# A masked softmax on one core: the first tile stored as three pieces (4, 4 and 8 rows per partition) instead of four (2, 2, 4 and 8)

## The chip, the core and the metric

The kernel runs on one core of a Trainium2 chip. The metric is the device time of one execution in microseconds: the median of several executions. A profiled execution gives a trace beside its time.

## The reference

The input `x` is 16 batches x 8 heads x 256 x 256 in float32; every batch has a length between 128 and 255. Each row is a softmax over its first `length` columns, and zero behind them.

```python
for b in range(batch):
    length = lengths[b]
    masked = x[b, :, :, :length].copy()
    masked = masked - np.max(masked, axis=-1, keepdims=True)
    exp_masked = np.exp(masked)
    result[b, :, :, :length] = exp_masked / np.sum(exp_masked, axis=-1, keepdims=True)
```

## The kernel before

A tile is one batch: 2048 rows of 256 floats, 16 rows in each of 128 partitions (`nt` = 16, `half` = 8, `quarter` = 4), 2 MB in all. A partition's 16 rows lie one behind the other in memory, in the input and in the output. Eight slots in SBUF (`xt`) hold tiles; position `b` in the order of work uses slot `b % 8`. There are 16 positions, 0 to 15. In this text a tile is named by its position (`batch_of`, L50, gives the batch).

Each tile goes through a load, a mask, an exponential with row sums, a division, and a store, in place:

- Loads. SP issues the load of tile 0 (L143). POOL issues those of tiles 1 to 3 as whole tiles (L194), and those of tiles 4 to 15 in a loop (L203, issue at L166), cut to a width that covers the batch's length, since the rest of the slot has been zeroed (L189). Before a load of the loop, POOL waits until the stores of the tile that had the slot are done (`s_st`, L207), and until the load two positions earlier has landed (`s_sw`, L165). So at most two of these loads are under way.
- Mask. VectorE takes the minimum of the data with a ramp that is far below zero behind the length (`clip`, L246). Tile 0 is masked in two halves, the others whole, so the third mask overall (`s_min` = 3) is that of tile 1.
- Exponential. ScalarE, one instruction for the first four rows (L372; VectorE sums these, L267), and one for each of the other twelve, which sums the row itself (L375).
- Division. VectorE takes reciprocals (L277) and multiplies, half a tile at a time (L280); each half raises `s_out` by 1.
- Store. SP, L144 to L154. `parts` (L59) cuts a tile into pieces, given in rows per partition. Every piece is one DMA of 128 partitions.

The order on VectorE is written out by hand (L287 to L300): both masks of tile 0, then for each tile the division of its first half, the mask of the next tile, the division of its second half, and the row sums of the next tile's first four rows. (For tile 1 the next mask comes first.) So the second half of tile `b` is divided after tile `b+1` has been masked, which needs the load of tile `b+1`.

SP runs through the stores in order. Before a piece it waits for the division of the half that holds the piece's last row (L147). Before the second piece of tile 0 it also waits for the third mask (L148, L149), and before the first piece of tiles 2 to 12 for the stores of the tile two positions earlier (L151). Behind the stores it waits for all of them (L155 to L157 and the end of the kernel). A store adds 16 for each piece of tile 0, and 16 for every four rows per partition of other tiles, so that each whole tile adds 64 (L154).

The last tiles: 13 and 14 are stored whole, 15 in two halves. Behind the last division VectorE checks that no sum was out of bounds (L315 to L326); a second pass that would repeat everything with the row maxima subtracted is not taken with these inputs.

Of the kernel before, what the change touches and what calls it, by code (L numbers as in the profile page):

```python
# [21 lines left out]
def kernel(  # L22
# [12 lines left out]
    nt = rows // P  # L35
    half = nt // 2
    quarter = nt // 4
# [12 lines left out]
    def batch_of(pos):  # L50
        return pos + 1 if pos < ahead - 1 else {ahead - 1: 15, 15: 0}.get(pos, pos)
# [7 lines left out]
    def parts(b):  # L59


        if b == 0:
            cuts = [0, 2, quarter, half, nt]
        elif b < 5:
            cuts = [0, half, half + quarter, nt]
        elif b < 13 or b == batch - 1:
            cuts = [0, half, nt]
        else:
            cuts = [0, nt]
        return [slice(i, j) for i, j in zip(cuts, cuts[1:])]  # L70
# [35 lines left out]
    with tc.tile_critical(sync_engine=POOL, no_gpsimd_drain=True):  # L106
# [37 lines left out]
        for b in range(batch):  # L144
            s_b = s_st[b % 2] if b < late else s_late if b < batch - 1 else s_last
            for s in parts(b):
                nc.sync.wait_ge(s_out, 2 * b + (s.stop - 1) // half + 1)  # L147
                if b == 0 and s.start == 2:  # L148
                    nc.sync.wait_ge(s_min, 3)  # L149
                if 2 <= b < late and s.start == 0:  # L150
                    nc.sync.wait_ge(s_b, 64 * (b // 2 + 2))  # L151
                nc.sync.dma_start(
                    out=out_f[batch_of(b), :, s, :], in_=xt[:, b % slots, s, :]
                ).then_inc(s_b, 16 * (1 if b == 0 else (s.stop - s.start) // quarter))  # L154
        for par in range(2):  # L155
            nc.sync.wait_ge(s_st[par], n_st[par])
        nc.sync.wait_ge(s_late, 64 * (batch - 1 - late))  # L157
# [45 lines left out]
        with nc.Fori(16, 16 * (batch // 2 - 1), 16, engines=[POOL]) as landed:  # L203
            for par in range(2):
                n = landed // 8 + (ahead - 2 + par)
                b = n % 15 if par == 1 else n
# [230 lines left out]
```

## Time and profile before

| what | value |
|---|---|
| median of 3 runs | 154.32 us (154.25 to 154.43) |
| the profiled execution | 154.43 us |
| its span in the trace | 152.8 us |
| VectorE busy | 134.7 us (88%) |
| ScalarE busy | 95.0 us (62%) |
| GpSimd (POOL) busy | 21.3 us (14%) |
| read from HBM, written to HBM | 27.98 MB, 33.55 MB |

The page has the busy time of each engine; a strip of 40 equal slices of the span, in which a digit is the busy share in tenths; the DMA queues (q1 is that of SP's transfers, q0 that of POOL's) with their packets, megabytes and the time of their packets as a share of 16 engines' time; and the transfers by size, with their count and, for loads, the median time from issue to landing. The rows of a queue can also be had for a stretch of the span alone; their share is then of 16 engines' time in that stretch. A timeline row has start, duration, engine, line, operation, and in brackets the idle time of the engine before it with what ended it. A row of a stretch (`a:b`) has its length, then for PE, weight loads, VectorE, ScalarE and POOL the busy time and the count of instructions, then the clock, the DMA share and GB/s. Times in the trace count from the start of the span.

### The profile page before, as it was taken

Reading aid. Unit: us, or ns where it says so; the run is one execution under the profiler, and the core shown is the slowest. Engines: PE = TensorE matmul, PEld = TensorE weight load, DVE = VectorE, ACT = ScalarE, POOL = GpSimd, SP = SyncE. Lnnn points to the kernel's source line nnn. Section 1 sums busy time; section 2 is a strip of 40 time slices with the busy share of each in tenths; the row PEclk is TensorE's granted clock in tenths of the full one; section 3 lists DMA queues with packets and bytes.
Section 4 is the critical chain, followed back from the end, with each engine's and each line's share of the span. In section 5 each row is a group of like instructions: output and inputs, shape, how many; then the busy total and the mean of one; then the engine's idle time right before and its main releaser. Section 6 shows DMA issues by size and latency. Waiting matters only on the chain.

```text
span 152.8 us, 817 instructions
## 1 busy us (share of the span) xinstructions
PE 0.3 (0%) x2; PEld 0.2 (0%) x2; DVE 134.7 (88%) x107; ACT 95.0 (62%) x402; POOL 21.3 (14%) x29
## 2 busy tenths in 40 slices
PE   0000000000000000000000000000000000000000
PEld 0000000000000000000000000000000000000000
DVE  1058999999999999999999999999999999889920
ACT  3019599808668493939486684939394866829200
POOL 4961110030303020030300303011030000000000
DMA  4999999999999999999999999999999999999993
GB/s 107 425 425 433 422 413 389 444 412 408 406 396 421 402 421 414 415 408 402 428 411 420 415 414 413 418 414 414 419 419 420 416 419 417 425 442 429 431 418 154
DMA packets 10070, 61.57 MB, mean 403 GB/s; under 512 B 834, under 2 KB 946, under 8 KB 6226
## 3 DMA queue, kind: packets, MB, share of 16 engines
q1 hardware_dynamic: 5328, 35.65, 56.7%
q0 software_dynamic: 4736, 25.89, 41.7%
q14 instruction: 4, 0.03, 0.1%
q10 hardware_dynamic: 2, 0.00, 0.0%
HBM read 27.98 MB, written 33.55 MB: 403 GB/s over the span
## 4 chain that ended last, share of the span: by engine, by line
DMA 82%; DVE 8%; issue 3%; POOL 1%; POOLq 1%; PE 0%; ACTq 0%
DMA xt<-in_x_dram 82%; DVE xt L280 5%; DVE xt L246 2%; POOL xt L189 1%; DMA word<-in_lengths_dram 1%; DVE row_sum L267 1%; POOLq L166 1%; DVE ends L315 0%; POOL xt L194 0%; DVE inv_sum L277 0%; DVE bad L318 0%; DVE len_s L237 0%; PE len_f L214 0%; PE count L216 0%; DVE len_b L234 0%
## 5 line engine op out<-in xcount | busy, mean ns | idle before, releaser
L375 ACT ACTIVATE xt<-xt 128x256 f32<-128x256 f32 x192 | 76.6, 400 | 0.0
L280 DVE TENSOR_TENSOR xt<-xt,inv_sum 128x2048 f32<-128x2048 f32 x32 | 73.4, 2292 | 1.1
L372 ACT ACTIVATE xt<-xt 128x1024 f32<-128x1024 f32 x16 | 16.9, 1057 | 45.7 <-DVE xt L246 45.7
L246 DVE SCALAR_TENSOR_TENSOR xt<-down,len_s,xt 128x2048 f32<-128x2048 f32 (+1 forms) x17 | 37.7, 2220 | 7.2 <-DMA xt<-in_x_dram 7.2
L375 ACT ACTIVATION_READ_ACCUMULATOR xt<-xt 128x1 f32 x192 | 35.9, 187 | 0.0
L166 POOL DMA_DIRECT2D xt<-in_x_dram x12 | 13.3, 1106 | 90.5 <-DMA xt<-in_x_dram 72.8
L267 DVE TENSOR_REDUCE row_sum<-xt 128x4 f32<-128x1024 f32 x16 | 19.4, 1212 | 0.0
L277 DVE RECIPROCAL inv_sum<-row_sum 128x8 f32<-128x8 f32 x32 | 6.4, 199 | 0.9 <-ACT xt L375 0.4
L189 POOL MEMSET xt<- 128x1536 f32 x4 | 5.4, 1398 | 1.1 <-DVE len_s L237 1.1
L359 ACT ACT_TABLE_LOAD x1 | 1.3, 1283 | 1.6 <-PEq L421 1.6
L194 POOL DMA_DIRECT2D xt<-in_x_dram x3 | 1.8, 591 | 0.0
L229 DVE TENSOR_SCALAR down<-iota_i 128x256 f32<-128x256 int32 x1 | 0.3, 301 | 1.6 <-POOL iota_i L179 1.6
L315 DVE TENSOR_REDUCE ends<-inv_sum 128x1 f32<-128x256 f32 x2 | 0.7, 408 | 0.0
L237 DVE TENSOR_SCALAR len_s<-len_f 128x16 f32<-128x16 f32 x1 | 0.2, 174 | 0.4 <-PE len_f L214 0.4
L216 PE MATMUL count<-bad,ones_c 128*1 128x3 bf16 x1 | 0.2, 165 | 143.4 <-DVE bad L318 143.4
L234 DVE CAST len_b<-word 1x16 bf16<-1x16 int32 x1 | 0.2, 163 | 0.4 <-DMA word<-in_lengths_dram 0.4
L179 POOL IOTA iota_i<- 128x256 int32 x1 | 0.3, 333 | 0.6 <-POOLq L106 0.6
L326 DVE TENSOR_REDUCE redo<-count 1x1 f32<-1x3 f32 x1 | 0.1, 150 | 0.3 <-PE count L216 0.3
L318 DVE TENSOR_SCALAR bad<-ends 128x1 bf16<-128x1 f32 x3 | 0.3, 150 | 0.0
L185 POOL MEMSET seed<- 1x1 f32 x2 | 0.2, 226 | 0.0
L216 PEld LDWEIGHTS count<-bad,ones_c 128*1 128x1 bf16 x1 | 0.1, 79 | 143.5 <-DVE bad L318 143.5
L359 ACT ACTIVATE warm<-const-float32-0.0 128x1 f32<-128x1 f32 x1 | 0.2, 203 | 0.0
(10 smaller groups left out, 1.1 us busy)
## 6 DMA issues: line engine op xcount, KB each, us to landing
out_dram<-xt SPq DMA_DIRECT2D x23, 1024.0 KB
xt<-in_x_dram POOLq DMA_DIRECT2D x4, 2048.0 KB, 16.5
xt<-in_x_dram POOLq DMA_DIRECT2D x3, 1728.0 KB, 18.2
out_dram<-xt SPq DMA_DIRECT2D x9, 512.0 KB
out_dram<-xt SPq DMA_DIRECT2D x2, 2048.0 KB
xt<-in_x_dram POOLq DMA_DIRECT2D x2, 1600.0 KB, 17.7
xt<-in_x_dram POOLq DMA_DIRECT2D x2, 1280.0 KB, 17.7
xt<-in_x_dram SPq DMA_DIRECT2D x1, 2048.0 KB, 8.2
```

What stands on the lines that cost most here:

```text
L166: nc.gpsimd.dma_start(out=xt[:, slot, :, :w], in_=x_n[:, b, :, :w]).then_inc(s_sw[par], 16)
L189: nc.gpsimd.memset(xt[:, b, :, low:], 0.0).then_inc(s_fill, 1)
L194: nc.gpsimd.dma_start(out=xt[:, b], in_=x_f[batch_of(b)]).then_inc(s_sw[b - 1] if b < 3 else s_ld[1], 16)
L216: nc.tensor.matmul(count, lhsT=ones_c, rhs=bad, start=True, stop=True).then_inc(s_count, 1)
L246: return nc.vector.scalar_tensor_tensor(out=t, in0=down[:, None, lo:hi].to_broadcast([P, s.stop - s.start, hi - lo]), scalar=len_s[:, batc ...
L267: nc.vector.tensor_reduce(out=row_sum[:, b % slots, :lump], in_=xt[:, b % slots, :lump, :], op=ALU.add, axis=AX,).then_inc(s_exp[0], 1)
L277: step(nc.vector.reciprocal(out=inv_sum[:, b, s], in_=row_sum[:, b % slots, s]))
L280: nc.vector.tensor_tensor(out=t, in0=t, in1=inv_sum[:, b, s, None].to_broadcast([P, half, seq_k]), op=ALU.mult,).then_inc(s_out, 1)
L315: step(nc.vector.tensor_reduce(out=ends[:, k : k + 1], in_=values, op=op, axis=AX))
L359: nc.scalar.activation(out=warm, in_=nc.const_aps.tensor(0.0, (P, 1), F32), func=EXP)
L372: nc.scalar.activation(out=e, in_=e, func=EXP).then_inc(s_lump, 1)
L375: ins = nc.scalar.activation(out=e, in_=e, func=EXP, accum_out=row_sum[:, slot, j : j + 1])
```

## The change

Tile 0 is cut at rows 4 and 8 instead of 2, 4 and 8: its first two pieces of 2 rows per partition (2 KB in each partition, 256 KB in all) become one piece of 4 rows (512 KB). The second piece, now rows 4 to 7, has the wait for the third mask that the piece from row 2 had. The semaphore's increments follow the general rule, so that tile 0 still adds 64. The instructions of the other engines are the same.

```diff
         if b == 0:
-            cuts = [0, 2, quarter, half, nt]
+            cuts = [0, quarter, half, nt]
...
-                if b == 0 and s.start == 2:
+                if b == 0 and s.start == quarter:
                     nc.sync.wait_ge(s_min, 3)
...
-                ).then_inc(s_b, 16 * (1 if b == 0 else (s.stop - s.start) // quarter))
+                ).then_inc(s_b, 16 * ((s.stop - s.start) // quarter))
```

## The prediction

> **What bounds the kernel now.** I read the page's DMA strip, queues and transfers first, then the DMA queues in chosen stretches, then the timeline of the last 20 us.
>
> ```profile
> span 152.8 us, 817 instructions
> DMA  4999999999999999999999999999999999999993
> DMA packets 10070, 61.57 MB, mean 403 GB/s; under 512 B 834, under 2 KB 946, under 8 KB 6226
> q1 hardware_dynamic: 5328, 35.65, 56.7%
> q0 software_dynamic: 4736, 25.89, 41.7%
> xt<-in_x_dram POOLq DMA_DIRECT2D x3, 1728.0 KB, 18.2
> xt<-in_x_dram SPq DMA_DIRECT2D x1, 2048.0 KB, 8.2
> out_dram<-xt SPq DMA_DIRECT2D x23, 1024.0 KB
> out_dram<-xt SPq DMA_DIRECT2D x9, 512.0 KB
> out_dram<-xt SPq DMA_DIRECT2D x2, 2048.0 KB
> out_dram<-xt SPq DMA_DIRECT2D x2, 256.0 KB
> ```
>
> The 16 DMA engines are full from the first slice to the last. q1 carries what SP issues: the first load and 36 stores, 37 transfers. 5328 / 37 = 144 packets each, for pieces of 256 KB and of 2048 KB alike: one per partition (128) and 16 small ones, one per DMA engine. So an engine's share of any SP transfer is 8 data packets and 1 small one, nine in all, whatever its size; a 2-row piece has packets of 2 KB, a 16-row piece of 16 KB. How do the queues share an engine? From 20 to 132 us, when both have work:
>
> ```profile
> q1 hardware_dynamic: 4373, 25.68, 55.7%
> q0 software_dynamic: 4350, 20.65, 45.8%
> ```
>
> 4373 packets against 4350, though the bytes differ by a quarter. It holds where the store packets are small (24 to 26 us, first pair below) and where they are large (124 to 129 us, second pair):
>
> ```profile
> q0 software_dynamic: 120, 0.57, 72.9%
> q1 hardware_dynamic: 121, 0.24, 30.5%
> ...
> q1 hardware_dynamic: 174, 1.29, 62.5%
> q0 software_dynamic: 172, 0.79, 39.8%
> ```
>
> The queues take turns packet by packet, and neither runs dry. So when the loads end depends on how many load packets there are, and on how large the store packets are that get the turns in between. The end of the loads matters here:
>
> ```profile
> DVE xt L246 <- DMA xt<-in_x_dram: 7.2, 2, 6.4
> 131.02 2.29 DVE L280 TENSOR_TENSOR xt<-xt,inv_sum 128x2048 f32<-128x2048 f32 x1
> 134.12 2.35 DVE L246 SCALAR_TENSOR_TENSOR xt<-down,len_s,xt 128x2048 f32<-128x2048 f32 x1 [0.81 <-DMA xt<-in_x_dram]
> 136.62 2.29 DVE L280 TENSOR_TENSOR xt<-xt,inv_sum 128x2048 f32<-128x2048 f32 x1
> 138.94 0.36 SPq L152 DMA_DIRECT2D out_dram<-xt  x1
> 142.63 0.36 SPq L152 DMA_DIRECT2D out_dram<-xt  x1
> 145.07 0.36 SPq L152 DMA_DIRECT2D out_dram<-xt  x1
> ```
>
> VectorE waits for loads twice, 6.4 us for the first tile and 0.81 us for the last one. The mask of tile 15 starts as its load lands, at 134.12. In VectorE's order it stands ahead of the second half of tile 14's division (136.62 to 138.91), and tile 14 is stored in one piece, issued at 138.94. So 134.12 + 4.82 = 138.94 is a chain without slack: last load, mask, division, store of tile 14. Is the store queue still supplied then?
>
> ```profile
> q1 hardware_dynamic: 489, 4.87, 82.6%
> 134.00:150.00 16.00, 0.17 (x1) 0.08 (x1) 11.94 (x15) 5.84 (x25) 0.00 (x0) 1.00 1.01 428
> 1.50:2.00 0.50, 0.00 (x0) 0.00 (x0) 0.30 (x1) 0.36 (x1) 0.48 (x5) 1.00 0.00 0
> 2.00:2.50 0.50, 0.00 (x0) 0.00 (x0) 0.16 (x1) 0.50 (x1) 0.00 (x0) 1.00 1.84 328
> 1.08 0.39 SPq L143 DMA_DIRECT2D xt<-in_x_dram  x1
> 150.00:150.50 0.50, 0.00 (x0) 0.00 (x0) 0.00 (x0) 0.00 (x0) 0.00 (x0) 1.00 0.74 311
> 150.50:151.00 0.50, 0.00 (x0) 0.00 (x0) 0.00 (x0) 0.00 (x0) 0.00 (x0) 1.00 0.16 66
> ```
>
> The first row is q1 from 138.94 to the end: 4.87 MB, of which tiles 14 and 15 are 4.19 MB (two of 128 x 16 KB). So 0.68 MB of tile 13 is left when tile 14 is issued, 0.68 / 428 GB/s = 1.6 us of work on the mean engine. A new transfer is not there at once: the first load was issued at 1.08, no bytes moved before 2.00 and some by 2.50, a lead of 0.9 to 1.4 us. Today the store of tile 14 arrives 0.2 to 0.7 us before the mean engine would be idle. That is all the cover.
>
> **The change, part by part.** 1. Two transfers of 256 KB become one of 512 KB: 16 packets of 2 KB and 2 small ones per engine become 8 packets of 4 KB and 1 small one. Prices of a data packet, as q1's share of 16 engines' time over its bytes: 2 KB from the 24 to 26 us row, 30.5% of 32 us = 9.76 us over 0.24 MB / 2048 = 117, 83 ns; 8 KB from the 124 to 129 us row, 62.5% of 80 us = 50.0 us over 1.29 MB / 8192 = 157, 317 ns. For 4 KB, 60 to 63 us:
>
> ```profile
> q1 hardware_dynamic: 153, 0.56, 46.5%
> ```
>
> 46.5% of 48 us = 22.3 us over 0.56 MB / 4096 = 137, 163 ns. Per engine 16 x 83 = 1.33 us against 8 x 163 = 1.30 us: the work itself shrinks by 0.02 us. I take nothing for it.
>
> 2. The turns. The same bytes of tile 0 now take nine turns fewer per engine. The load packets are as many as before, so when the last of them has had its turn, the store stream stands nine turns further on. What those nine turns are is read where the loads end: q1 from 134.12 on.
>
> ```profile
> q1 hardware_dynamic: 678, 6.99, 87.9%
> ```
>
> 6.99 MB less tiles 13 to 15 (6.29 MB) leaves 0.70 MB of tile 12's second half, so the loads end among 8 KB packets. Nine turns there are 8 x 317 ns and a small one: 2.5 us. The last load lands about 2.5 us later, at 136.6. Bounds: nothing, if turns are not what decides; 8 x 317 plus one packet of tile 13 (16 KB, twice 317) in place of one of 8 KB, 2.9 us. I take 2.5, since the counts of turns agree to 0.5% over 112 us.
>
> 3. What is late next. Mask of tile 15 at 136.6, tile 14's store at 138.94 + 2.5 = 141.4. VectorE adds nothing: even if mask 14 were 2.5 us late too, it would be free at 133.3 + 2.5 = 135.8. The DMA engines have by then moved the same bytes as before, so tile 13 is finished when it was, and they run dry. The loss is 2.5 us less the cover. The cover of the mean engine is 0.2 to 0.7 us; but the engines do not finish together. Their share is 0.74 in the half microsecond after 150.00 and 0.16 in the next, a mean end of 150.45, while the last ends near 151.0 to 151.3, so the engine that sets the end has 0.6 to 0.8 us more: 0.8 to 1.5 us. I take 1.3, toward the top, since a lead of about 1 us is where the first bytes appear. Net +1.2 us, from 1.0 to 1.7 by the cover alone and to 2.1 with 2.9 us of delay.
>
> 4. The waits. The first piece goes at the same time, since both need the first division. The second still waits for the third mask:
>
> ```profile
> 15.95 0.35 SPq L152 DMA_DIRECT2D out_dram<-xt  x1
> 18.28 0.34 SPq L152 DMA_DIRECT2D out_dram<-xt  x1
> q1 hardware_dynamic: 81, 0.17, 10.6%
> ```
>
> The last row is 19 to 23 us: 0.17 MB, less than the first 0.26 MB piece. What is issued at 18.28 lies in the queue until 23 at least, 4.7 us of cover; with a larger first piece, more. SP issues one instruction less there (0.34 us), hidden by the same queue. Loads on POOL's queue take 18.2 us from issue to landing where 1728 KB move in some 9.6 us (20.65 MB in 112 us), so the next load is queued 8 us ahead and the delay does not grow through POOL's waits.
>
> Sum: 154.43 (the profiled execution; 152.8 span and 1.63 around it) + 1.2 = 155.6; it stands 0.11 above the median of the runs, so on the median 155.5.
>
> **A rule against this reckoning.** 37 times 144 packets means one packet per partition row, 2 KB or 16 KB. The Trainium skill, DMA: Bandwidth & Descriptors, section "SWDGE vs HWDGE vs iDMA", gives a packet as at most 4096 B preferably, up to 64 descriptors, as the unit of switching; by it two 2 KB rows could share a turn. The page's count of packets does not agree. The result that it would give is the first rival.
>
> **The rivals.** *Not slower: the small packets share turns.* If two 2 KB packets went in one turn, the two old pieces cost 4 + 4 data turns and 2 small ones, the new one 8 and 1. One turn is saved; the stores stand one 8 KB packet ahead, 0.3 us at the last load, and the cover of 0.8 to 1.5 us hides it: 154.4. The rows 121 against 120 at 24 to 26 us, with 2 KB packets, speak against it. The same time results if a load queue that ran dry somewhere re-set the lag; 4373 against 4350 shows no room for that. Chance 0.12.
>
> *Faster: a transfer's fixed cost comes off.* If what precedes a transfer's first bytes were exposed for the second piece, one such lead of 0.9 us would go: 153.5. Against it, the strip is full at 15 to 25 us. The Trainium skill, the same page, section "Rules for kernel authors", asks for 1 MiB or more per DMA, and its fit of 2.0 us per transfer would take 2.0 us off, 152.4. Chance 0.08.
>
> *Slower by all of it.* If the store of tile 14 has no cover, because a transfer into an idle queue starts slower than 0.9 us or the late engines are late from there on: 154.43 + 2.5 = 156.9. The 0.68 MB left at 138.94 speaks against it. Chance 0.10.
>
> **How the numbers follow.** Turns as reckoned: 0.70, 155.5, own range 155.1 to 156.1 (cover and delay as bounded). The range 154.3 to 156.3 takes in the first rival and leaves out the fast one and most of the slowest. About 0.2% (0.31 us) is what a measurement can tell from no change. Faster: the fast rival and a tail of the first, 0.09. Same: most of the first and a tail of the main case, 0.12. Slower: 0.79.
>
> **What would show it.** Right: q1 has 5184 packets; packets of the queues still equal between 20 and 132 us; VectorE's wait before the mask of tile 15 grows from 0.81 to some 3 us, the mask starts near 136.6; tile 14's store is issued near 141.4; and the DMA share dips between 140 and 143 us, where it is full now. Wrong: the last mask stays at 134.1 (turns do not decide); or it moves and the strip has no dip (more cover than I count); or the loss lies elsewhere, as in POOL waiting longer for stores.

## The result and the profile after

| | before | after |
|---|---|---|
| median (6 runs each) | 154.37 us | 155.12 us |
| the profiled execution | 154.43 us | 155.12 us |
| its span | 152.8 us | 153.5 us |

The ratio is 1.0046, with a 95% interval of 1.0036 to 1.0055: slower by 0.7 us. The prediction was 155.5, with 0.79 on slower.

The page of the kernel after: the DMA strip, the packets, and the two queues.

```profile
span 153.5 us, 816 instructions
DMA  4999999999999999999999999999999999997995
DMA packets 9926, 61.57 MB, mean 401 GB/s; under 512 B 818, under 2 KB 930, under 8 KB 6082
q1 hardware_dynamic: 5184, 35.65, 56.5%
q0 software_dynamic: 4736, 25.89, 41.6%
```

The megabytes are those of before. q1 has 5184 packets, 36 x 144 instead of 37 x 144. The strip has one new gap, a 7 at the fourth slice from the end (slices of 3.84 us, so 138.2 to 142.0 us). The queues between 20 and 132 us:

```profile
q1 hardware_dynamic: 4276, 26.04, 56.3%
q0 software_dynamic: 4267, 20.30, 45.2%
```

Packets are as even as before (4276 against 4267), but in the same 112 us the stores have moved 0.36 MB more (26.04 against 25.68) and the loads 0.35 MB less (20.30 against 20.65). That is what one store turn of each pair having a larger packet looks like. VectorE's waits for loads come next, then the end of VectorE's work and the store of tile 14 in the timeline:

```profile
DVE xt L246 <- DMA xt<-in_x_dram: 9.2, 3, 6.3
136.24 2.35 DVE L246 SCALAR_TENSOR_TENSOR xt<-down,len_s,xt 128x2048 f32<-128x2048 f32 x1 [1.71 <-DMA xt<-in_x_dram]
138.74 2.29 DVE L280 TENSOR_TENSOR xt<-xt,inv_sum 128x2048 f32<-128x2048 f32 x1
141.06 0.36 SPq L152 DMA_DIRECT2D out_dram<-xt  x1
```

The mask of tile 15 starts at 136.24 instead of 134.12, and tile 14's store is issued at 141.06 instead of 138.94: both 2.12 us later. The DMA engines meanwhile, in stretches around that issue and at the end (the last two columns are DMA share and GB/s; a packet counts whole in the stretch in which it starts):

```profile
140.00:140.50 0.50, 0.00 (x0) 0.00 (x0) 0.50 (x1) 0.50 (x4) 0.00 (x0) 1.00 0.77 328
140.50:141.00 0.50, 0.00 (x0) 0.00 (x0) 0.50 (x2) 0.50 (x3) 0.00 (x0) 1.00 0.24 98
...
141.06:141.80 0.74, 0.00 (x0) 0.00 (x0) 0.74 (x1) 0.74 (x5) 0.00 (x0) 1.00 0.00 0
141.80:141.90 0.10, 0.00 (x0) 0.00 (x0) 0.10 (x1) 0.10 (x2) 0.00 (x0) 1.00 0.38 164
...
150.00:151.00 1.00, 0.00 (x0) 0.00 (x0) 0.00 (x0) 0.00 (x0) 0.00 (x0) 1.00 1.07 442
151.00:151.50 0.50, 0.00 (x0) 0.00 (x0) 0.00 (x0) 0.00 (x0) 0.00 (x0) 1.00 0.74 311
151.50:152.00 0.50, 0.00 (x0) 0.00 (x0) 0.00 (x0) 0.00 (x0) 0.00 (x0) 1.00 0.64 262
```

The stores before tile 14 run out: their last packets start between 140 and 141, and no new one starts until 141.80 to 141.90, 0.74 to 0.84 us behind the issue. This is the dip.

### The profile page after: what moved, and what is told of

Same layout as the page of the kernel before. It is cut to its first block, busy times and chain, and to the rows that moved or that the text cites. A ratio compares the mean times of both kernels' runs of the same rounds, so it can differ in the third digit from the quotient of the medians.

```text
span 153.5 us, 816 instructions
## 1 busy us (share of the span) xinstructions
PE 0.3 (0%) x2; PEld 0.2 (0%) x2; DVE 134.8 (88%) x107; ACT 95.0 (62%) x402; POOL 21.3 (14%) x29
## 3 DMA queue, kind: packets, MB, share of 16 engines
q1 hardware_dynamic: 5184, 35.65, 56.5%
## 4 chain that ended last, share of the span: by engine, by line
DMA 83%; DVE 8%; issue 3%; POOL 1%; POOLq 1%; PE 0%; ACTq 0%
DMA xt<-in_x_dram 83%; DVE xt L280 4%; DVE xt L246 2%; POOL xt L189 1%; DMA word<-in_lengths_dram 1%; DVE row_sum L267 1%; POOLq L166 1%; DVE ends L315 0%; POOL xt L194 0%; DVE inv_sum L277 0%; DVE bad L318 0%; DVE len_s L237 0%; PE len_f L214 0%; PE count L216 0%; DVE len_b L234 0%
```

## The experiments

Each edit is against the kernel after, but for two that say "kernel before". The runs of the kernel before beside them had medians of 154.30 to 154.37 us.

**The same number of packets, another shape.** Tile 0 in four pieces of 4 rows.

```diff
-            cuts = [0, quarter, half, nt]
+            cuts = [0, quarter, half, half + quarter, nt]
```

> Tile 0 in four pieces of 4 rows (4, 4, 4, 4) instead of the changed kernel's 4, 4, 8: 36 turns per DMA engine, as many as the kernel before has for 2, 2, 4, 8, with the same large first piece as the changed kernel. Theory of turns: the number of packets counts, not their size, so the last load lands as in the kernel before: mask of tile 15 at 134.1 (within 0.3), tile 14's store at 138.9, no dip of the DMA share at 140 to 143 us; time 154.4, ratio to before 1.000 (0.998 to 1.002). Rival, the large first piece itself: a first piece of 512 KB that takes bandwidth from the loads of tiles 2 and 3 does the harm; then 155.1, ratio 1.0046, as with the change.

Measured: 154.41 us, ratio 1.0006 (0.9997 to 1.0014). The last mask, in the timeline:

```profile
133.68 2.35 DVE L246 SCALAR_TENSOR_TENSOR xt<-down,len_s,xt 128x2048 f32<-128x2048 f32 x1 [0.26 <-DMA xt<-in_x_dram]
138.50 0.37 SPq L152 DMA_DIRECT2D out_dram<-xt  x1
```

The mask is a little earlier still than the bound of 134.1 less 0.3, and there is no dip (the DMA share is 0.95 to 1.08 in each microsecond from 140 to 143). The 512 KB first piece is there and the loss is gone, so the rival falls: what counts is the number of packets. As every transfer of SP has 144 of them, this run alone can't tell nine packets per engine from one transfer; that packets are what takes turns rests on the rows where both queues move equal counts.

**The nine turns put back in another tile.** Tile 1 as 4, 4, 4, 4.

```diff
+        elif b == 1:
+            cuts = [0, quarter, half, half + quarter, nt]
         elif b < 5:
```

> The changed kernel, with tile 1 stored as 4, 4, 4, 4 instead of 8, 4, 4: the nine turns per engine that tile 0 lost are put back in another tile, some 10 us later. Theory of turns: as the kernel before, 154.4, mask of tile 15 at 134.1 (within 0.3), ratio 0.998 to 1.002. Rival, the first tile's own shape (what happens from 16 to 29 us is what counts): 155.1, ratio 1.0046, mask of tile 15 at 136.2.

Measured: 154.41 us, ratio 0.9999 (0.998 to 1.0019).

```profile
134.24 2.35 DVE L248 SCALAR_TENSOR_TENSOR xt<-down,len_s,xt 128x2048 f32<-128x2048 f32 x1 [0.89 <-DMA xt<-in_x_dram]
139.05 0.37 SPq L154 DMA_DIRECT2D out_dram<-xt  x1
```

As before the change (134.12, 138.94). It does not matter that the turns lie in tile 0.

**Nine turns fewer still.** Tile 1 as 8, 8.

```diff
+        elif b == 1:
+            cuts = [0, half, nt]
         elif b < 5:
```

> The changed kernel, with tile 1 stored as 8, 8 instead of 8, 4, 4: nine more turns per engine are gone. Theory of turns: the last load is later by another 2.1 to 2.5 us, mask of tile 15 at 138.3 to 138.7; the cover is used up by the first nine turns, so all of it shows in the time: 155.1 + 2.1 to 2.5 = 157.2 to 157.6, ratio 1.018 to 1.021. Rival, the first tile's own shape: no change against the changed kernel, 155.1. Rival, larger transfers are better: under 155.1.

Measured: 155.84 us, ratio 1.0098 (1.0083 to 1.0113). The direction is that of the turns, the size is a third: 0.7 us where 2.1 to 2.5 were expected. The timeline first (the masks of tiles 14 and 15; tile 13's store with the three behind it, merged; tile 14's store), then the queues at 133 to 134, 134 to 135 and 135 to 136 us:

```profile
128.23 2.35 DVE L248 SCALAR_TENSOR_TENSOR xt<-down,len_s,xt 128x2048 f32<-128x2048 f32 x1 [3.23 <-DMA xt<-in_x_dram]
136.95 2.35 DVE L248 SCALAR_TENSOR_TENSOR xt<-down,len_s,xt 128x2048 f32<-128x2048 f32 x1 [0.23 <-DMA xt<-in_x_dram]
133.05 15.21 SPq L154 DMA_DIRECT2D out_dram<-xt  x4
141.77 0.36 SPq L154 DMA_DIRECT2D out_dram<-xt  x1
```

```profile
q1 hardware_dynamic: 33, 0.27, 65.0%
q0 software_dynamic: 33, 0.15, 38.0%
...
q0 software_dynamic: 47, 0.22, 54.7%
q1 hardware_dynamic: 31, 0.16, 40.0%
...
q0 software_dynamic: 71, 0.24, 62.2%
q1 hardware_dynamic: 21, 0.25, 58.1%
```

Up to 132 us the rule held: from 20 us on POOL's queue has moved 4194 packets here, 4267 with the change and 4350 before it, so the first nine turns put it back by 83 packets and the second nine by 73. Then tile 14's load was late too: its mask waited 3.23 us and began at 128.23. Tile 13 is stored whole behind it, so this store went out only at 133.05. At 134 to 136 us the store queue moved few packets (31 and 21 against 47 and 71), the loads got more than every second turn, and the last one caught up. The mask of tile 15 is only 0.71 us later than with the change (136.95), tile 14's store as well (141.77), and the time 0.72 us. So mask, store and time move together, more closely than traces of like kernels agree (their masks differ by up to 0.6 us); that each nine turns cost the last load the same does not hold here.

The late issue alone does not explain it. Packet by packet in the trace, tile 12's last store packets end between 134.47 and 135.65 on the sixteen engines, but tile 13's first one starts only at 135.28, 2.2 us behind its issue. Its first eleven packets start at 135.28, 135.30, 135.38 and so on to 135.78, and the closing small packets of the last load end at 135.28, 135.31, 135.39 and so on to 135.78, each within 0.01 us of such a start. So an engine began the new store when its own share of the load was done. Why this store got no turns before that stays open.

**The tail's wait taken away.** Tile 14 in halves.

```diff
-        elif b < 13 or b == batch - 1:
+        elif b < 13 or b >= batch - 2:
             cuts = [0, half, nt]
```

> The changed kernel, with tile 14 stored in two halves instead of whole, so that its first half, which is divided ahead of the mask of tile 15, can leave before the last load has landed. Theory: the mask of tile 15 stays late (136.2, within 0.3), but the dip at 140 to 142 us is filled with the first half (about 2.5 us of store work), and the whole loss comes back: 154.2 to 154.5, ratio 0.998 to 1.001. Rival, the loss lies ahead of the tail (a worse mix of loads and stores): 155.1, ratio 1.0046.

Measured: 154.44 us, ratio 1.0003 (0.9995 to 1.0012). The last mask, the two stores of tile 14, and the DMA engines where the dip was:

```profile
136.18 2.35 DVE L246 SCALAR_TENSOR_TENSOR xt<-down,len_s,xt 128x2048 f32<-128x2048 f32 x1 [1.77 <-DMA xt<-in_x_dram]
134.44 0.36 SPq L152 DMA_DIRECT2D out_dram<-xt  x1
141.00 0.37 SPq L152 DMA_DIRECT2D out_dram<-xt  x1
140.00:141.00 1.00, 0.00 (x0) 0.00 (x0) 1.00 (x2) 1.00 (x6) 0.00 (x0) 1.00 0.91 385
141.00:142.00 1.00, 0.00 (x0) 0.00 (x0) 1.00 (x1) 1.00 (x7) 0.00 (x0) 1.00 1.01 426
```

The load is as late as with the change, the dip is filled, and the time is that of before. The whole loss arose in the dip; the late load in itself costs nothing. This kernel has 5328 packets on q1 again, but its extra nine turns lie behind the last load (from 20 to 132 us q1 has 4277, as with the change), so it is not the total that counts.

**The kept wait.** Without the wait for the third mask.

```diff
-                if b == 0 and s.start == quarter:
-                    nc.sync.wait_ge(s_min, 3)
```

> The changed kernel without the wait of the second piece of tile 0 for the third mask (it may be issued as soon as the first half is divided). Theory: the piece lies in the store queue behind the first one anyhow, whose packets move until about 24.8 us, so the wait costs and gives nothing: 155.1, ratio to before 1.0046 (1.003 to 1.006), mask of tile 15 at 136.2 (within 0.3). Rival, the wait keeps stores back to the loads' good: slower than 155.1 by 0.3 or more, last load later.

Measured: 155.10 us, ratio 1.0049 (1.0036 to 1.0063), with the last mask at 136.30. SP now issues both pieces one right behind the other (merged in this row):

```profile
15.89 0.88 SPq L150 DMA_DIRECT2D out_dram<-xt  x2
```

The second piece goes out at 16.29 instead of 18.20, and these 1.9 us change nothing. The wait is idle here.

**Nine turns more than before.** The kernel before, with tile 1 as 4, 4, 4, 4 (the edit of the second experiment).

> The kernel before, with tile 1 stored as 4, 4, 4, 4 instead of 8, 4, 4: nine turns per DMA engine more than before. Theory: the last load lands 2 to 2.5 us earlier (near 131.7), but VectorE is free for the mask of tile 15 only at 133.3, and the DMA engines had no dip to fill: mask of tile 15 at 133.3 without a wait, time 154.4, ratio 0.998 to 1.002. Rival, the time follows the last load in both directions: 0.7 us or more faster, 153.7 or less.

Measured: 154.38 us, ratio 1.0005 (0.9996 to 1.0014). Its queue, and VectorE's only wait for a load, that for the first tile:

```profile
q1 hardware_dynamic: 5472, 35.65, 56.8%
DVE xt L248 <- DMA xt<-in_x_dram: 6.3, 1, 6.3
```

5472 is 38 x 144. The mask of tile 15 starts at 133.15 without a wait, 1 us earlier than before. The last packet of POOL's queue ends at 131.61 in this trace and at 133.67 in that of the kernel before: nine turns move the last load by 2.1 us in this direction too. Nothing comes of it: with full DMA engines an earlier load only leaves more stores for the end.

**The kernel before, with tile 14 in halves.**

> The kernel before, with tile 14 stored in halves. Theory: the DMA engines have no dip at 140 to 143 us there, so there is nothing to fill: 154.3 to 154.45, ratio 0.998 to 1.001. Rival, some engines are already idle for part of the 0.2 to 0.7 us by which the store comes early on the mean engine: 0.2 to 0.4 us faster, 154.0 to 154.2.

Measured: 154.39 us, ratio 1.0004 (0.9995 to 1.0013). There was no dip to fill, and no idle share that this could recover.

**Both late stores in halves.** Tile 1 as 8, 8, and tiles 13 and 14 in halves.

```diff
+        elif b == 1:
+            cuts = [0, half, nt]
         elif b < 5:
             cuts = [0, half, half + quarter, nt]
-        elif b < 13 or b == batch - 1:
-            cuts = [0, half, nt]
         else:
-            cuts = [0, nt]
+            cuts = [0, half, nt]
```

> The kernel with tile 0 as 4, 4, 8 and tile 1 as 8, 8 (eighteen turns fewer than before), and tiles 13 and 14 stored in halves instead of whole. Theory: there the loss of 1.5 us arose in the tail alone, where the store queue ran dry twice (tile 13's store behind the mask of tile 14, at 133 to 136 us, and tile 14's behind the mask of tile 15, at 140 to 142.5); the first halves fill both. The mask of tile 15 comes later still (137.5 to 138.7, since the loads no longer get the turns of a dry store queue), and the time returns to 154.2 to 154.7, ratio 0.998 to 1.002. Rival, late loads cost as such or the larger transfers do: 155.8 or more.

Measured: 156.25 us, ratio 1.0129 (1.0113 to 1.0145), far above the 154.2 to 154.7 expected. The last mask, the last four stores, and the DMA engines:

```profile
138.65 2.35 DVE L246 SCALAR_TENSOR_TENSOR xt<-down,len_s,xt 128x2048 f32<-128x2048 f32 x1 [1.76 <-DMA xt<-in_x_dram]
136.92 0.36 SPq L152 DMA_DIRECT2D out_dram<-xt  x1
143.47 0.36 SPq L152 DMA_DIRECT2D out_dram<-xt  x1
147.17 0.37 SPq L152 DMA_DIRECT2D out_dram<-xt  x1
149.61 0.37 SPq L152 DMA_DIRECT2D out_dram<-xt  x1
143.00:144.00 1.00, 0.00 (x0) 0.00 (x0) 1.00 (x2) 1.00 (x7) 0.00 (x0) 1.00 0.14 57
144.00:148.00 4.00, 0.00 (x0) 0.00 (x0) 3.90 (x5) 2.88 (x15) 0.00 (x0) 1.00 0.63 262
```

The mask came where it was expected (138.65): with tile 13's first half in the queue, issued at 133.23, the queues stay even (76 packets against 74 from 134 to 136 us) and the loads no longer catch up. It is 2.41 us later than with the change, so here the second nine turns cost their full price. But the dip was not filled, it was moved behind 143 us: the remaining stores follow VectorE one by one. The expectation had counted one chain from the last mask, to tile 14's second half (4.82 us), and not the other, to the last half of tile 15: 149.61 - 138.65 = 10.96 us, then 0.84 us to the first bytes (the upper end of 0.74 to 0.84) and an estimated 2.45 us for 1 MB (at the 428 GB/s of before). In the kernel with tile 14 in halves that sum is 136.18 + 14.25 = 150.4, ahead of the 151.0 to 151.3 at which the DMA engines of the kernel before end; here it is 152.9.

**Between the two.** Tile 1 as 8, 8 and tile 14 alone in halves.

> Tile 0 as 4, 4, 8, tile 1 as 8, 8 (eighteen turns fewer than before, as in the merge of tile 1 that took 155.84), and tile 14 alone in halves, tile 13 whole. Theory of two chains from the mask of tile 15: to tile 14's second half (4.8 us), and to the last half of tile 15 (issued 10.96 us after the mask starts, then 0.84 us to its first packet and 2.45 us for 1 MB). With tile 13 whole the store queue is dry at 134 to 136 us and the loads catch up, so the mask of tile 15 starts at 136.9 to 137.0; tile 14's first half fills the hole at 140 to 142.5; the second chain moves its last data at 136.95 + 14.25 = 151.2, where the kernel before ends too. Time 154.3 to 154.6, ratio 0.999 to 1.003. Rival, late loads or larger transfers cost as such: 155.8 or more; rival, the halves of tile 14 keep the loads late as the halves of 13 and 14 did: mask at 138.6 and 156.2.

Measured: 154.69 us, ratio 1.0033 (1.0015 to 1.005), just above the 154.3 to 154.6 expected. Last mask, last store, and the stretch in which the DMA engines are not full:

```profile
137.22 2.35 DVE L248 SCALAR_TENSOR_TENSOR xt<-down,len_s,xt 128x2048 f32<-128x2048 f32 x1 [0.22 <-DMA xt<-in_x_dram]
148.17 0.36 SPq L154 DMA_DIRECT2D out_dram<-xt  x1
145.00:146.00 1.00, 0.00 (x0) 0.00 (x0) 0.97 (x3) 0.45 (x3) 0.00 (x0) 1.00 0.61 254
```

The mask is 0.27 us later than in the kernel with tile 13 whole and tile 14 whole (136.95). By the second chain 137.22 + 14.25 = 151.5 us, 0.3 behind the 151.2 at which the data of before end by the expectation's count; the time is 0.34 us longer. Eighteen turns fewer cost 0.3 us with this tail, and 1.5 us with tile 14 whole. No version was faster than the kernel before by more than the interval of its ratio.

## Why the prediction was right

**Turns, not bytes, decide when the loads end.** Right, and shown: three kernels of quite different shape (before, tile 0 or tile 1 as 4, 4, 4, 4), with 4373 to 4376 packets on q1 from 20 to 132 us, take 154.37 to 154.41 us; the changed kernel, with 4276, takes 155.12; and the loads lose in bytes what the stores gain. The total over the whole run does not decide: with tile 14, or tiles 13 and 14, in halves it is 5328 too, and the last load is late all the same. The rule has one exception: the store of tile 13 that got no turns beside the last load (tile 1 as 8, 8). The rule by which two 2 KB rows could share a turn, and with it the first rival, is out: then the change would have cost the last load 0.3 us instead of 2.1.

**The delay of the last load.** Predicted 2.5 us, measured 2.12 between the two traces (134.12 to 136.24). Three traces with the old number of turns before that point have the last mask at 134.12, 133.68 and 134.24, three with nine fewer at 136.24, 136.18 and 136.30: means of 134.01 and 136.24, 2.2 us apart. (A fourth of the old number, the kernel before with tile 14 in halves, starts it at 133.77 without a wait, so its start is no measure of the load.) So some of the difference is one trace against another; the rest, 0.3 us, stays open.

**The store of tile 14 and the dip.** Right: issued at 141.06 (141.4 predicted), dip between 140 and 142 us, and both go when the first half may leave early.

**The cover.** Predicted 1.3 us, between 0.8 and 1.5; measured 2.12 less the 0.7 by which the span grew, 1.4 us. Both of its parts can be read, packet by packet, from the traces: the last packets of the sixteen engines end between 149.98 and 151.29 before (mean 150.56), and between 151.82 and 151.98 after (mean 151.89). The mean moved by 1.3 us, so the mean engine had 0.8 of cover (0.2 to 0.7 predicted; the lead of a transfer into an idle queue was bounded by 0.9 to 1.4 us from the first load, and this store shows 0.74 to 0.84). The last engine moved by 0.7, so 0.6 came from the ends evening out (0.6 to 0.8 predicted).

**The sum.** The net of 1.2 us came out as 0.7, less than the 1.0 that the sum gave as its least by the cover: 0.4 us of the difference is the delay, for which the sum had no value between nothing and 2.5, and 0.1 the cover. The chain was right, this term was too large. That 155.12 us lies inside the own range of 155.1 to 156.1, by a hair, is partly luck: by the sum's bounds the range would begin at 154.3 + 1.0 = 155.3.

**The waits.** The kept wait at nothing: shown. VectorE's wait before mask 15 grew to 1.71 us and not to some 3, because mask 14 was late as well and waited 1.20 us (three waits instead of two); the sum had this covered as harmless. POOL's waits for stores, a sign that the prediction had named against itself, rose. The pairs are before, after, and the changed kernel with tile 14 in halves:

```profile
POOL xt L166 <- DMA xt<-in_x_dram: 72.8, 10, 12.5
POOL xt L166 <- DMA out_dram<-xt: 7.7, 1, 7.7
...
POOL xt L166 <- DMA xt<-in_x_dram: 42.2, 6, 14.7
POOL xt L166 <- DMA out_dram<-xt: 39.6, 5, 9.2
...
POOL xt L166 <- DMA xt<-in_x_dram: 72.5, 10, 14.5
POOL xt L166 <- DMA out_dram<-xt: 9.2, 1, 9.2
```

They are not where the loss lies. A later landing and a later store end are two waits of the same loop, and a wait is put down to whichever came last: the two add up to 80.5, 81.8 and 81.7 us, and the third kernel has the late load of the change with hardly any wait for stores. The queue below never ran dry (4267 packets). The fast rival (a transfer's fixed cost) is out: 38, 37, 36 and 35 transfers from SP take 154.38, 154.37, 155.12 and 155.84 us, no gain from fewer.

## What to carry to other kernels

In this kernel loads and stores share full DMA engines and take turns by packets, so the cut of a store is a weight: more and smaller pieces slow the stores and speed the loads, at the same total. Where a trace shows equal packet counts on two queues, find who waits for the last load, how many bytes of other work the queue holds at that moment, and count the lag in packets. A piece that need not wait for that load (half of tile 14 here) gave back the whole loss, while no cut of tiles 0 and 1 beat the kernel before. And look for the next chain from the same load before spending the cover.

## What was not expected of the hardware

The 16 small packets of each transfer count as turns. The packets of both queues from 20 to 132 us match with these included (4375 against 4362 with tile 0, 4376 against 4338 with tile 1 as 4, 4, 4, 4); without them, a ninth, q1 would have some 3890 of the 4376.

After a dip the engines end together. In the changed kernel the last packets of the sixteen engines end within 0.16 us of each other, before it within 1.31: the pause lines the engines up. The other traces agree. In the four other kernels with a gap in the tail (tile 1 as 8, 8; without the wait; both with tile 1 as 8, 8 and halves) the ends lie within 0.13 to 0.17 us, in the five others without one within 0.7 to 1.6.

A store that was issued beside a busy load queue did not get its turns at once: tile 13's, stored whole at 133.05 in the kernel with tile 1 as 8, 8, and at 133.34 in the one that has tile 14 in halves besides, began on each engine about when that engine's loads were done, from 135.28 and 135.38 us on. A store of half a tile at 133.23 kept even turns. The runs do not show why.
